# Attention's query tiles in a one-core hybrid block: who writes their constant rows

## The chip, the cores and the metric

The kernel runs on one core of one Trainium2 chip. The metric is device time in microseconds of one execution. Before the change three timed executions took 3047.77, 3050.18 and 3064.09 us; the median, 3050.18 us, is the time that the change is measured against.

## The reference

One layer over 16 meta tokens and 2048 frames of width 1024: an RMS norm and an input projection, three groups of heads side by side (RG-LRU, forgetting attention, RWKV-7), an output projection with norm and residual, then a gated feed-forward network. The part that matters here is the attention, 8 heads of 64:

```python
c = jnp.cumsum(log_f, axis=1)                       # log forget gates, summed over time
s = einsum('bhqd,bhkd->bhqk', qb, kh) + (cb[..., :, None] - c[..., None, :])
s = jnp.where(kpos[None, :] <= qpos[:, None], s, -jnp.inf)
p = jax.nn.softmax(s, axis=-1)
o = einsum('bhqk,bhkd->bhqd', p, vh)
```

## The kernel before, in words

The program has four stages on one core. Stage one multiplies the normed input by the input weights and runs the two recurrences beside it (class Rwkv and the LRU). Its last projection matmul is at 890 us of the span. Stage two is the attention (class `Attn`), from there to about 1580 us, with the rest of the recurrences and most of the output projection beside it. Stage three is the first half of the feed-forward network, stage four its second half.

Every matrix product of float32 values is done in parts: a value is split into a rounded high part and a low rest, and the products of the parts are summed. For attention this is packed into the contraction dimension of 128 partitions. A score tile (`sc`, lines 681 and 682) is the sum of two matmuls, `k1` by `q1` and `k2` by `q2`. A maximum tile (`mx`, line 554) is one matmul, `q3` by `k2`, of which only the row maximum is used. Partitions 0 to 63 of `q3` and `q2` hold a head's queries. Partitions 64 to 127 hold constants or zero: in `q3` partition 64 is 0, partitions 65 and 66 are 1 (they add the two parts of the forget sum that stand in the same partitions of `k2`), and the rest is 0. In `q2` all are 0 at first, and partition 64 later gets the negative row maximum from ScalarE (line 568). In `k2` partition 64 is 1, partitions 65 and 66 are loaded, and the rest is 0.

These tiles are allocated once, in `Attn.__init__`, as rings of three `q3`, three `q2` and two `k2`, and reused for all 32 steps (8 heads by 4 blocks of 512 queries), so the constant rows are written once. VectorE writes them for the queries: lines 476, 477 and 478 in the helper `fixed` for each `q3` (64 partitions of 0, then 3 of 1, then 1 of 0) and line 462 for each `q2`. GpSimd writes them for `k2` (lines 480 and 481).

A step is made of `maxima` (up to five `mx` pieces for each of four query tiles, each followed by a VectorE row maximum at line 559; then a reduction at 564, transposes at 567 and the ScalarE operation at 568) and `weights` (scores, exponentials at line 686, sums and values). `maxima` runs two steps ahead of `weights` (`AHEAD = 2`).

The order of instructions within each engine isn't the order of the code. A scheduler in the framework plays the program through and gives each engine a list that it then runs in that order; every DMA named here is issued by SyncE (SP), in order as well. So the recurrences and the attention are merged on every engine, and an instruction that is taken away lets the scheduler place all that follows anew.

The names that the prediction uses beside these: `rwst` is the recurrence's state, which line 1267 (VectorE) copies and line 1263 (TensorE) multiplies, four times in turn for each block of 256 frames; `rwix` at line 78 is the last of a square root's steps and the input of the matmul at line 1067; `rwraw` (line 996) is a load of projection rows for the next block of the recurrence, and line 1006 (ScalarE) and 1007 (VectorE) read it; `rww` at line 1313 is the normed output of a recurrence block, which line 1320 (TensorE) transposes; line 1179 is the recurrence's triangular solve, whose results go through VectorE (lines 1189, 1195, 1202) and come back.

Of the kernel before, what the change touches and what calls it, by code (L numbers as in the profile page):

```python
# [8 lines left out]
F32 = mybir.dt.float32  # L9
# [3 lines left out]
AF = mybir.ActivationFunctionType  # L13
# [5 lines left out]
P = 128  # L19
# [13 lines left out]
class Core:  # L33


    def __init__(self, tc, ctx):
        self.tc = tc
        self.nc = tc.nc
        self.ctx = ctx
        self.uid = 0  # L40
        nc = self.nc
        self.const = ctx.enter_context(tc.tile_pool(name="const", bufs=1))
        self.ident = self.const.tile([P, P], F32, name="ident")
        make_identity(nc, self.ident[:])
        self.flip = 0
        self.root = self.apart = False
# [310 lines left out]
def attn_consts(core):  # L357
    nc = core.nc
    c = core.const

    core.future = c.tile([META, META], F32, name="future")
    core.futureb, core.identb = (c.tile([P, P], BF16, name=s) for s in ("futureb", "identb"))
    for t, n in ((core.future, META), (core.futureb, P)):
        nc.gpsimd.memset(t[:], 0.0)
        nc.gpsimd.affine_select(
            out=t[:], in_=t[:], compare_op=ALU.is_ge, fill=NEG, base=0, pattern=[[-1, n]], channel_multiplier=1
        )
    nc.vector.tensor_copy(core.identb[:], core.ident[:])
    core.ones_row = c.tile([1, P], F32, name="ones_row")
    nc.vector.memset(core.ones_row[:], 1.0)  # L370
    core.ccol = c.tile([P, NKT, NH], F32, name="ccol")
    nc.vector.memset(core.ccol[:], 0.0)
    core.cref = c.tile([P, NKT, NH], F32, name="cref")
    core.ncref = c.tile([1, NKT, NH], F32, name="ncref")
    core.ctail = c.tile([NH, META], F32, name="ctail")
    nc.vector.memset(core.ctail[:], 0.0)
    core.ones_col = c.tile([P, 1], F32R, name="ones_col")
    nc.vector.memset(core.ones_col[:].bitcast(F32), 1.0)
    core.ones_64 = c.tile([META, 64], F32, name="ones_64")
    nc.vector.memset(core.ones_64[:], 1.0)  # L380
    core.ones_8 = c.tile([NH, 1], F32, name="ones_8")
    nc.vector.memset(core.ones_8[:], 1.0)

# [55 lines left out]
class Attn:  # L439
# [7 lines left out]
    def __init__(self, core, pool, psum, more, scr):  # L447
        self.core, self.pool, self.psum, self.more, self.scr = core, pool, psum, more, scr
        self.wide, self.bank, self.place = False, 0, 0
        nc = self.nc = core.nc  # L450
        self.clock, self.later, self.serial, self.added = 0, [], 0, 0
        self.pending, self.loads, self.steps, self.beside = None, [], [], iter(())


        self.turn = {"k": 1, "q2": 0, "q3": 0}
        self.ring = {s: [] for s in self.turn}
        for i in range(self.AHEAD + 1):
            q3 = pool.tile([P, 512], F32R, tag=f"q3_{i}", name=core.n("q3"), bufs=1)
            self.fixed(q3, None, self.ONES)
            self.ring["q3"].append(q3)  # L460
            q2 = pool.tile([P, 512], F32R, tag=f"q2_{i}", name=core.n("q2"), bufs=1)
            nc.vector.memset(q2[64:128].bitcast(F32), 0.0)
            self.ring["q2"].append(q2)
            if i > 1:
                continue
            k1 = pool.tile([P, 2, KHALF], F32R, tag=f"k1_{i}", name=core.n("k1"), bufs=1)
            k2 = pool.tile([P, 2, KHALF], F32R, tag=f"k2_{i}", name=core.n("k2"), bufs=1)
            v1 = pool.tile([P, 2, NKT // 2 + 1, 64], F32, tag=f"v1_{i}", name=core.n("v1"), bufs=1)
            self.fixed(None, k2, self.ONES)
            self.ring["k"].append((k1, k2, v1))  # L470
# [1588 lines left out]
def hybrid_block_kernel(ctx: ExitStack, tc: tile.TileContext, args, out):  # L2059
# [25 lines left out]
    with ExitStack() as p1:  # L2085
# [7 lines left out]
        with ExitStack() as p1a:  # L2093
# [6 lines left out]
            for part in range(3):  # L2100
# [9 lines left out]
                if part == 0:  # L2110
                    attn_consts(core)
                    rk = rwkv_consts(
                        core, gp, ps_ae,
                        {
                            s[5:]: (v.rearrange("h d -> (h d)") if s == "rwkv_r_k" else v)
                            for s, v in a.items() if s.startswith("rwkv_")
                        },
                    )
                    lk = lru_consts(
                        core, gp, ps_ae,  # L2120
                        {
                            "conv_w": a["lru_conv_w"], "conv_b": a["lru_conv_b"], "ga_w": a["lru_gate_a_w"],
                            "ga_b": a["lru_gate_a_b"], "gx_w": a["lru_gate_x_w"], "gx_b": a["lru_gate_x_b"],
                            "lam": a["lru_lambda"],
                        },
                    )
                    columns(core, gp, ps_ae, [a["ffn_conv"].rearrange("i (r p) -> (i r) p", p=P)], "", cw)
                    R = Rwkv(core, rp, dp, ps_rw, ps_ae, scr, rk)
                    beside = Beside(PACE)
# [190 lines left out]
```

## Time and profile before

| | |
|---|---|
| three timed executions, us | 3047.77, 3050.18, 3064.09 |
| the profiled execution, us | 3044.26 |
| its span, first to last instruction, us | 3042.5 |
| granted TensorE clock, mean | 0.977 |
| TensorE busy, 890 to 940 us | 36.36 of 50 us |
| TensorE busy, 1300 to 1400 us | 97.00 of 100 us |
| VectorE busy, 890 to 940 us | 42.56 of 50 us |

How to read the lines of the profile: in a timeline row come the start in us, the duration in us, engine, line, operation, output and inputs with their sizes, the count, and in brackets how long the engine stood idle before it and what ended that. In a table by windows come, for each stretch of time, the busy microseconds and instruction counts of TensorE (PE), its weight loads (PEld), VectorE (DVE), ScalarE (ACT) and GpSimd (POOL), the granted TensorE clock, the share in which the DMA engines were busy, and what they moved in GB/s. Rows of a line's own view give the shortest, median and longest duration in ns, and the first and last start. A row of waits gives total, count and longest.

### The profile page before, as it was taken

The page shows a single profiled execution, that of the slowest core. Times are in us where ns is not written, and L with a number is a line of the kernel's source. Part 1 is how long each engine was busy: PE and PEld are TensorE (multiplying, and loading weights), DVE is VectorE, ACT ScalarE, POOL GpSimd, SP SyncE. Part 2 cuts the span into 40 slices and gives each one's busy share as a digit, 9 for nine tenths or more (in the row PEclk, how much of TensorE's full clock was granted, in tenths as well). Part 3 has the DMA queues.
Part 4 walks back from the last instruction along what each step waited for, and adds up shares of the span by engine and source line. Part 5 has one row for each costly group of instructions (what it writes and reads, how often), then busy time and mean ns, then how long its engine had stood idle before and what let it go on. Part 6 is the DMA issues. An engine that isn't in the chain of part 4 may idle for free. (4 is left out here: it accounts for less than half of the span.)

```text
span 3042.5 us, 52754 instructions
## 1 busy us (share of the span) xinstructions
PE 2901.8 (95%) x18694; PEld 2486.7 (82%) x18694; DVE 2043.7 (67%) x3947; ACT 1480.9 (49%) x2858; POOL 1309.2 (43%) x1567
## 2 busy tenths in 40 slices
PE   6998999999989998999989899999999999999998
PEld 6998898888876654565568899999999999787887
DVE  5268645656677885555736888888778777646666
ACT  4245342434346654454634656666666665434333
POOL 1001121122224656566843457545655544556443
PEclk9998999999998999999999999999999999999999
DMA  6776478565654347434326555567677764536453
GB/s 211 245 233 214 155 237 294 159 212 193 213 160 95 97 102 214 110 94 123 82 81 221 166 168 181 180 187 221 210 220 208 216 204 130 167 109 213 146 182 120
DMA packets 469189, 530.48 MB, mean 174 GB/s; under 512 B 85710, under 2 KB 355736, under 8 KB 467372
## 3 DMA queue, kind: packets, MB, share of 16 engines
q1 hardware_dynamic: 468156, 526.17, 56.6%
q8 instruction: 147, 2.41, 0.3%
q0 software_dynamic: 768, 0.93, 0.1%
q14 instruction: 118, 0.97, 0.1%
HBM read 368.07 MB, written 158.90 MB: 173 GB/s over the span
## 5 line engine op out<-in xcount | busy, mean ns | idle before, releaser
L172 PE MATMUL psu<-xo,uw 128*128 128x344 f32 x1848 | 591.3, 324 | 15.6 <-DVE vb L1812 7.9
L173 PE MATMUL psu<-xo,uw 128*128 128x344 f32 x1848 | 593.9, 322 | 0.0
L174 PE MATMUL psu<-xo,uw 128*128 128x344 f32 x1848 | 585.0, 321 | 0.7 <-DVE uw L1621 0.7
L172 PE MATMUL psp<-xh,wh 128*128 128x384 f32 (+2 forms) x1152 | 382.9, 332 | 4.2 <-ACT wh L166 3.1
L174 PE MATMUL psp<-xh,wl 128*128 128x384 f32 (+2 forms) x1152 | 380.3, 331 | 2.0 <-DMA wl<-scr_wk 1.8
L173 PE MATMUL psp<-xl,wh 128*128 128x384 f32 (+2 forms) x1152 | 379.5, 330 | 0.0
L172 PEld LDWEIGHTS psu<-xo,uw 128*128 128x128 f32 x1848 | 348.1, 189 | 19.1 <-DVE vb L1812 9.9
L1621 DVE TENSOR_TENSOR uw<-uq,uw 128x512 fp32r<-128x512 f32 x341 | 316.9, 936 | 67.9 <-ACT uw L1620 65.8
L173 PEld LDWEIGHTS psu<-xo,uw 128*128 128x128 f32 x1848 | 349.2, 189 | 0.0
L174 PEld LDWEIGHTS psu<-xo,uw 128*128 128x128 f32 x1848 | 347.7, 189 | 1.3 <-DVE uw L1621 1.2
L1620 ACT ACTIVATE uw<-uq 128x512 fp32r<-128x512 f32 x462 | 287.0, 627 | 105.0 <-PE psu L174 47.8
L686 ACT ACTIVATE p<-sc,bias 128x512 f32<-128x512 f32 (+4 forms) x352 | 197.4, 590 | 191.3 <-PE sc L682 159.1
L559 DVE TENSOR_REDUCE mc<-mx 128x1 f32<-128x512 f32 (+6 forms) x352 | 190.3, 564 | 105.2 <-PE mx L554 79.9
L1760 DVE SCALAR_TENSOR_TENSOR uy<-psu,ffn_cols,uy 128x342 f32<-128x342 f32 (+1 forms) x390 | 220.2, 566 | 57.4 <-ACT uy L1758 55.7
L1768 POOL TENSOR_TENSOR uy<-uy,uy 128x342 f32<-128x342 f32 (+1 forms) x132 | 139.3, 1056 | 249.8 <-DVE uy L1760 63.7
L1621 POOL TENSOR_TENSOR uw<-uq,uw 128x512 fp32r<-128x512 f32 x121 | 180.9, 1495 | 148.4 <-ACT uw L1620 130.5
L725 POOL TENSOR_TENSOR acc<-acc,p 128x512 f32<-128x512 f32 (+3 forms) x208 | 221.2, 1066 | 52.3 <-DVE acc L725 26.3
L174 PEld LDWEIGHTS psp<-xh,wl 128*128 128x128 f32 x1152 | 221.3, 192 | 11.5 <-issue 6.0
L172 PEld LDWEIGHTS psp<-xh,wh 128*128 128x128 f32 x1152 | 221.4, 192 | 11.0 <-issue 4.0
L173 PEld LDWEIGHTS psp<-xl,wh 128*128 128x128 f32 x1152 | 221.2, 192 | 7.7 <-issue 5.6
L1621 DVE TENSOR_TENSOR fo<-u,fo 128x896 fp32r<-128x896 f32 x88 | 100.1, 1138 | 132.7 <-ACT fo L1620 132.2
L1620 ACT ACTIVATE fo<-u 128x896 fp32r<-128x896 f32 x88 | 81.2, 923 | 207.1 <-PE psd L174 115.6
(483 smaller groups left out, 6399.2 us busy)
## 6 DMA issues: line engine op xcount, KB each, us to landing
uq<-scr_us SPq DMA_DIRECT2D x220, 256.0 KB
uq<-in_ffn_up_dram SPq DMA_DIRECT2D x209, 256.0 KB
wl<-scr_wk SPq DMA_DIRECT2D x48, 512.0 KB
wh<-scr_wk SPq DMA_DIRECT2D x48, 512.0 KB
u<-scr_ff SPq DMA_DIRECT2D x88, 256.0 KB
scr_ff<-uy SPq DMA_DIRECT2D x110, 171.0 KB
raw<-in_w_in_dram SPq DMA_DIRECT2D x24, 512.0 KB
scr_wk<-wh SPq DMA_DIRECT2D x24, 512.0 KB
```

The source lines that it names most:

```text
L172: nc.tensor.matmul(out, ah, bh, start=first, stop=False, skip_group_check=more)
L173: nc.tensor.matmul(out, ah, bl, start=False, stop=False, skip_group_check=more)
L174: nc.tensor.matmul(out, al, bh, start=False, stop=last, skip_group_check=more)
L559: self.reduced = nc.vector.tensor_reduce(mc[:rows, i, ci : ci + 1], ps[:rows, : e - a], axis=AX.X, op=ALU.max)
L686: last = nc.scalar.activation(p[:rows, :w], ps[:rows, :w], AF.Exp, bias=bias[:rows, j : j + 1])
L725: eng.tensor_tensor(a, ps_[0][0][:rows, c0:n] if start and i == 1 else a, p[:rows, : n - c0], op=ALU.add)
L1620: core.nc.scalar.activation(hi, src, AF.Copy)
L1621: (eng or core.nc.vector).tensor_tensor(lo, src, hi, op=ALU.subtract)
L1760: core.conved = stt(y[:, :n], src[:, i : n + i], cw[:, 44 * i + cc : 44 * i + cc + 1], y[:, :n], op0=ALU.mult, op1=ALU.add)
L1768: core.pooled = nc.gpsimd.tensor_tensor(v[:, :n], g[:, :n], v[:, :n], op=ALU.mult)
```

## The change

`attn_consts` gets a column of 128 values, `qrows`, written by three VectorE memsets of one column at the start of the program: 0 everywhere, 1 in partitions 64 to 66, 0 in partition 64. In `Attn.__init__` the three memsets of each `q3` give way to one ScalarE operation that multiplies any finite input by 0 and adds the column as its bias. The memset of each `q2` moves from VectorE to GpSimd. `fixed` stays, for the `k2` tiles and for the 16 meta tokens.

```diff
+    core.qrows = c.tile([P, 1], F32, name="qrows")
+    for rows, value in ((slice(0, P), 0.0), (slice(64, 64 + Attn.ONES + 2), 1.0), (slice(64, 64 + Attn.ONES), 0.0)):
+        nc.vector.memset(core.qrows[rows], value)
...
             q3 = pool.tile([P, 512], F32R, tag=f"q3_{i}", name=core.n("q3"), bufs=1)
-            self.fixed(q3, None, self.ONES)
+            nc.scalar.activation(
+                q3[64:128], core.ident[64:128, 0:1].to_broadcast([64, 512]), AF.Identity, scale=0.0,
+                bias=core.qrows[64:128],
+            )
             self.ring["q3"].append(q3)
             q2 = pool.tile([P, 512], F32R, tag=f"q2_{i}", name=core.n("q2"), bufs=1)
-            nc.vector.memset(q2[64:128].bitcast(F32), 0.0)
+            nc.gpsimd.memset(q2[64:128].bitcast(F32), 0.0)
```

The lines of the changed kernel are numbered 3 higher from line 381 on and 6 higher from line 463 on. Up to the start of the attention the order of every engine is that of before, but for the three small memsets and a few constants set around them. From there to about 1500 us of the span the scheduler has placed much anew; behind that, the orders are the same again. Three places follow.

VectorE where the attention begins, before. The names `q_1455`, `q_1460` and `q_1465` are the three `q3`; `q_1456`, `q_1461` and `q_1466` are the three `q2`; `mc` collects maxima.

```order
L1267 COPY rwst_9235<-rps_9237 128x128
L476 MEMSET q_1455_11123 64x512
L462 MEMSET q_1456_11127 64x512
L476 MEMSET q_1460_11134 64x512
L462 MEMSET q_1461_11138 64x512
L476 MEMSET q_1465_11145 64x512
L77 TENSOR_TENSOR rwitmp_9683<-rwitmp_9683,rwia_9681 4x256
L462 MEMSET q_1466_11149 64x512
L547 MEMSET mc_11168 128x20
L547 MEMSET mc_11204 128x20
L1267 COPY rwst_9235<-rps_9237 128x128
L477 MEMSET q_1455_11123 3x512
```

The same place of the changed kernel, with line 1273 for 1267 and 1075 for 1069.

```order
L1273 COPY rwst_9239<-rps_9241 128x128
L553 MEMSET mc_11166 128x20
L553 MEMSET mc_11202 128x20
L77 TENSOR_TENSOR rwitmp_9687<-rwitmp_9687,rwia_9685 4x256
L78 SCALAR_TENSOR_TENSOR rwix_9686<-rwitmp_9687,rwix_9686 4x256
L1273 COPY rwst_9239<-rps_9241 128x128
L1176 STREAM_TRANSPOSE rwxu_9972<-rwxu_9972 64x512
L1075 SCALAR_TENSOR_TENSOR rwk_9660<-rwk_9660,rwkv_cols,eps_9773 128x256 x2
```

The twelve memsets (five more of them stand behind the rows shown) are gone, and the second state copy has moved up past all those that stood ahead of it. The three ScalarE operations stand behind the last rounding of the projection (line 234), ahead of the three bias operations (line 570 before, 576 now). The three GpSimd memsets stand among those of `k2`: one `q2`, one `k2`, and so on, and then the rows of 1.

SyncE in the same stretch, before: the query loads of the third step, the values, the keys of the next head, and then the recurrence's `rwraw`.

```order
L541 DMA q_1455_11123<-scr_qh 64x512
L542 DMA q_1495_11264<-scr_qh 64x512
L543 DMA q_1495_11264<-scr_qh 64x512
L544 DMA q_1456_11127<-scr_ql 64x512
L523 DMA v_1459_11131<-scr_v 128x8x64
L524 DMA v_1459_11131<-scr_v 16x64
L523 DMA v_1459_11131<-scr_v 128x8x64
L524 DMA v_1459_11131<-scr_v 16x64
L515 DMA k_1463_11141<-scr_kh 64x1040
L517 DMA k_1463_11141<-scr_ch 1x1040
L518 DMA k_1463_11141<-scr_cl 1x1040
L996 DMA rwraw_10432<-scr_p 128x2x65
```

The changed kernel, with line 1002 for 996, 525 and 526 for 519 and 520, 547 for 541.

```order
L525 DMA k_1457_11131<-scr_kh 64x1040
L1002 DMA rwraw_10436<-scr_p 128x2x65
L526 DMA k_1457_11131<-scr_kl 64x1040
L547 DMA q_1455_11127<-scr_qh 64x512
L548 DMA q_1495_11262<-scr_qh 64x512
L549 DMA q_1495_11262<-scr_qh 64x512
L550 DMA q_1456_11129<-scr_ql 64x512
L529 DMA v_1459_11133<-scr_v 128x8x64
```

`rwraw` has moved up by twelve loads, past the third step's queries and the values.

TensorE at the recurrence's first triangular solve within the attention, before.

```order
L1179 MATMUL rps_10039<-rwxu_9968,rwsc_8714 32x32 x32
L554 MATMUL mx_11381<-k_1458_11130,q_1460_11134 128x400
L554 MATMUL mx_11384<-k_1458_11130,q_1460_11134 128x512
L556 LDWEIGHTS identb
L556 MATMUL mx_11384<-futureb,identb 128x128
L681 MATMUL sc_11462<-q_1495_11264,k_1457_11129 128x512
L682 MATMUL sc_11462<-q_1456_11127,k_1458_11130 128x512
L681 MATMUL sc_11468<-q_1495_11264,k_1457_11129 128x400
L682 MATMUL sc_11468<-q_1456_11127,k_1458_11130 128x400
L1179 MATMUL rps_10073<-rwxu_9968 32x32 x16
```

The changed kernel, with line 1185 for 1179, 560 for 554, 573 for 567, 687 and 688 for 681 and 682.

```order
L1185 MATMUL rps_10043<-rwxu_9972,rwsc_8718 32x32 x32
L573 MATMUL mx_11312<-ident,sh_11310 1x128 x4
L560 MATMUL mx_11337<-k_1458_11132,q_1460_11136 128x400
L687 MATMUL sc_11414<-q_1477_11197,k_1457_11131 128x272
L688 MATMUL sc_11414<-q_1466_11147,k_1458_11132 128x272
L687 MATMUL sc_11420<-q_1477_11197,k_1457_11131 128x144
L688 MATMUL sc_11420<-q_1466_11147,k_1458_11132 128x144
L1185 MATMUL rps_10077<-rwxu_9972 32x32 x16
```

The solve stands earlier among the attention's rows, and between its first two parts stand 1,744 streamed columns where 2,864 stood.

## Prediction

> **What bounds the kernel now.** I read the page's table of busy time first.
>
> ```profile
> span 3042.5 us, 52754 instructions
> PE 2901.8 (95%) x18694; PEld 2486.7 (82%) x18694; DVE 2043.7 (67%) x3947; ACT 1480.9 (49%) x2858; POOL 1309.2 (43%) x1567
> ```
>
> TensorE is busy for 95% of the span, so an edit on VectorE counts only where TensorE waits for it. The second view is the table by windows around 890 us, where the attention begins.
>
> ```profile
> 896.00:900.00 4.00, 0.90 (x10) 0.71 (x10) 3.35 (x10) 0.00 (x0) 3.15 (x2) 0.72 1.00 238
> 900.00:904.00 4.00, 2.84 (x6) 1.66 (x6) 3.49 (x9) 0.00 (x0) 0.00 (x0) 0.50 0.91 215
> 904.00:908.00 4.00, 4.00 (x38) 2.70 (x37) 3.44 (x10) 0.00 (x0) 0.00 (x0) 0.50 0.91 227
> ...
> 916.00:920.00 4.00, 2.76 (x10) 2.25 (x11) 3.17 (x15) 2.46 (x5) 0.53 (x3) 0.50 1.19 210
> 920.00:924.00 4.00, 3.98 (x20) 2.75 (x19) 3.90 (x8) 2.08 (x6) 3.61 (x8) 0.80 1.15 213
> 892.00:928.00 36.00, 23.68 (x200) 16.86 (x196) 30.68 (x85) 8.08 (x17) 11.69 (x14) 0.76 0.96 198
> 925.00:1580.00 655.00, 609.04 (x3635) 375.84 (x3635) 414.49 (x942) 345.24 (x669) 410.38 (x573) 0.96 0.43 110
> ```
>
> From 892 to 928 us TensorE does 23.68 of 36 us, at a mean clock of 0.76, while VectorE is busy for 30.68 and the DMA engines are full. This seam is bound by VectorE and by the loads, not by TensorE. From 925 to 1580 us TensorE stands idle for 655 - 609.04 = 46 us; there it is the bound. The third view is the timeline of TensorE in the seam.
>
> ```profile
> 898.15 0.70 PE L1263 MATMUL rps<-rwst,rwgt 64*64 64x64 f32 x8 [3.79 <-DVE rwst L1267]
> 901.16 2.07 PE L1067 MATMUL eps<-rwix,spr 4*128 4x256 f32 x4 [2.11 <-DVE rwix L78]
> 907.40 0.91 PE L554 MATMUL mx<-k,q 128*128 128x144 f32 x1
> 917.24 0.58 PE L554 MATMUL mx<-k,q 128*128 128x256 f32 x1 [2.66 <-ACT q L568]
> ```
>
> Two waits of 3.79 and 2.11 us end on the state copy and on the square root, both on VectorE. The fourth view says what VectorE did instead.
>
> ```profile
> L476 DVE MEMSET q<- x3: 485/485/485, 894.0 to 896.2; 64x512 f32 x3
> L462 DVE MEMSET q<- x3: 485/485/485, 894.6 to 897.3; 64x512 f32 x3
> L477 DVE MEMSET q<- x3: 485/485/485, 898.3 to 900.2; 3x512 f32 x3
> L478 DVE MEMSET q<- x3: 485/485/485, 901.3 to 902.8; 1x512 f32 x3
> 897.83 0.27 DVE L1267 COPY rwst<-rps 128x128 f32<-128x128 f32 x1
> 900.69 0.41 DVE L78 SCALAR_TENSOR_TENSOR rwix<-rwitmp,rwix 4x256 f32<-4x256 f32 x1
> ```
>
> A memset of 1 partition takes as long as one of 64. The twelve sit exactly between the copies and the root that TensorE waits for.
>
> **The change part by part: what goes.** VectorE loses 12 x 0.485 = 5.82 us in the seam. TensorE's two waits there are 3.79 + 2.11 = 5.90 us, so the two views agree on the size: what follows can come forward by 5.8 us at most. Whether it does depends on what is late next.
>
> ```profile
> 894.25 0.47 SPq L515 DMA_DIRECT2D k<-scr_kh  x1
> k<-scr_kh SPq DMA_DIRECT2D x8, 260.0 KB
> q<-scr_qh SPq DMA_DIRECT2D x13, 128.0 KB
> ```
>
> First, the loads. The first maxima (907.40 us) need `k2` and `q3`; ahead of them in the queue lie two loads of 260 KB and, as long again, the low part, then 128 KB: 908 KB beside the small rows. The first is issued at 894.25; at the 238 GB/s of the window from 896 us that is 3.8 us, so some time about 899 to 901 us. The maxima would come at 907.40 - 5.8 = 901.6 us. The loads allow it, with little to spare.
>
> Second, ScalarE's part of the step, which now is late for another reason.
>
> ```profile
> 909.29 0.91 ACT L1006 ACTIVATE rwrav<-rwraw,rwkv_om 128x256 f32<-128x256 f32 x2 [18.12 <-PE rps L1295]
> 916.14 0.35 ACT L1006 ACTIVATE rwwa<-rwraw,rwkv_om 128x64 f32<-128x64 f32 x1 [2.13 <-DMA rwraw<-scr_p]
> 916.51 0.68 ACT L568 ACTIVATE q<-mx,ncref 1x512 fp32r<-1x512 f32 x1
> 912.00 0.38 SPq L996 DMA_DIRECT2D rwraw<-scr_p  x1
> rwraw<-scr_p SPq DMA_DIRECT2D x1, 65.0 KB
> ```
>
> The row maximum at 916.51 us, on which the first full scores depend, stands behind a ScalarE operation that waits for `rwraw`, loaded 4.1 us after its issue. If that load stayed at 912.00, the gain would end here. It doesn't: it has moved up past twelve loads on SyncE, 65 KB ahead of the low keys and the third step's queries. Those are wanted well behind 917 us, so I count the move itself at nothing.
>
> Third, TensorE's new order. The transposes of line 1320 now stand ahead of the scores with 272 columns, and they need the recurrence's normed output.
>
> ```profile
> 920.41 1.53 DVE L1313 TENSOR_TENSOR rww<-rww,rwgsm 128x512 f32<-128x512 f32 x1
> ```
>
> VectorE reaches that product only behind a chain of ten small operations and several row maxima. Before, six score and maximum matmuls more stood ahead of the transposes. I take 1.5 us, the length of that product, as newly exposed. The bounds are 0, if the maxima cover it, and 3 us, twice the row. So the seam gives 5.8 - 1.5 = 4.3 us, between 2.8 and 5.8.
>
> **What comes.** Three ScalarE operations over 64x512, and three GpSimd memsets.
>
> ```profile
> L748 ACT ACTIVATE oh<-acc x32: 612/618/632, 936.1 to 1565.7; 128x512 fp32r<-128x512 f32 x32
> L1165 POOL MEMSET rwxu<- x9: 195/523/527, 12.0 to 1059.4; 64x512 f32 x8, 64x128 f32 x1
> 895.55 3.60 POOL L481 MEMSET k<- 1x2080 f32 x2
> ```
>
> ScalarE's nearest row is 0.618 us, so 1.9 us for the three; they lie in the 18.12 us for which ScalarE stands idle ahead of 909.29. Without that cover they would cost 1.9 us, but no queue is behind them there. On GpSimd three memsets of 0.523 us delay the last constants of `k2` from 899.15 to 900.7 us. The first maxima wait for those, at 901.6 us in the sum above: covered by 0.9 us, at most 1.6 us if the cover is gone. The three memsets of one column at the program's start cost VectorE a fraction of a microsecond while loads are awaited. All this is counted at nothing.
>
> **The new order behind the seam.** About 570 us of attention run in another order. It has the same work, and TensorE's idle 46 us are the sum of many short waits.
>
> ```profile
> PE sc L681 <- ACT p L686: 9.5, 18, 2.0
> PE mx L554 <- DVE mc L559: 7.2, 9, 2.7
> PE mx L751 <- ACT oh L748: 7.0, 2, 4.7
> ```
>
> Whether a wait of this kind falls away or comes new can't be read from the order. I take 0, and as bounds one of these three groups more or less, 9.5 us either way. The handover to the feed-forward network has the order of before, so a gain reaches the end unshortened.
>
> **The sum.** The profiled execution took 3044.3 us; less 4.3 is 3040.0. The median lies 5.9 us above it, and I expect the changed kernel's runs to do likewise: 3045.9 us, a gain of 0.14%. A measurement of this kernel tells apart about 0.5%, 15 us.
>
> **One rule weighed.** The granted clock falls to 0.72 in the window with the 3.79 us wait and to 0.50 in the next. The Trainium skill (TensorE: Matmul & The Clock Gate, section "Part 1: The HAM clock gate (the "warmup" mystery)") says that a window of about 3.4 us without activity halves TensorE's clock and a busy one of that length restores it. The trace agrees. By that rule the seam without its waits would run at full clock, and the sum would be the second rival's. I don't count it, since TensorE then waits for its first keys for about as long.
>
> **The rivals.** *The loads take over* (3050 us): TensorE gets ready earlier and then waits for keys and queries; for it speaks a DMA share of 0.91 to 1.19 in the windows shown from 896 to 924 us, against it the 899 to 901 us worked out above. The gain is then under 1 us.
>
> *The clock stays up* (3039 us): the whole 5.8 us, and the 2.84 + 4.00 us of matmuls between 900 and 908 us, granted 0.50, run at twice the clock, which saves 3.4 us; the 2.76 us between 916 and 920 save 1.4 more. 3050.2 - 10.6 = 3039.6. Against it speaks the wait for the first loads.
>
> *The recurrence in TensorE's way* (3062 us): the solve now stands earlier, with 1,744 columns instead of 2,864 between its first parts, and TensorE runs in order.
>
> ```profile
> 948.28 3.19 PE L1179 MATMUL rps<-rwxu 32*32 32x32 f32 x96 [1.65 <-DVE rwxu L1189]
> ```
>
> Three blocks of the recurrence are left, with about ten such turns each through VectorE or ScalarE. Should ten of thirty become exposed at 1.65 us, that costs 16.5 us, and 3045.9 + 16.5 = 3062. It eats the gain from three exposed turns on (4.3 / 1.65). Against it: over the whole first solve the columns between its parts come to about the same, some are thinner and some thicker.
>
> *The operation is not free* (3048 us): the ScalarE form calls for a table load, 1.28 us each at line 1431, and the `q3` are late. The lists of both kernels hold 52 table loads and none at this place, so this is all but excluded.
>
> ```profile
> L1431 ACT ACT_TABLE_LOAD  x18: 1283/1283/1283, 214.2 to 1049.1; - x18
> ```
>
> **How the numbers follow.** Forecast (3041 to 3050) 0.50, loads 0.20, recurrence 0.16, clock 0.12, operation 0.02. The range goes from the clock's 3039 less most of the 9.5 us of the order, 3032, up to 3060: the forecast plus 9.5 and the spread of the three timings, without the worse part of the recurrence's case. Faster by over 0.5% means below 3034.9: only the clock's case with luck in the order, or the forecast with all of it, 0.11. Slower means above 3065.4: a third of the recurrence's case and a bad order, 0.09. That leaves 0.80 for the same.
>
> **What would show it.** Right: the four state copies lie under 2 us apart, TensorE's first maxima start before 903 us, the row maximum on ScalarE before 912 us, and the attention's last stage starts 4 us earlier. Wrong: the first maxima behind 905 us with no VectorE wait ahead (the loads); waits of line 1185 on VectorE over 5 us in total (the recurrence); TensorE's idle time from 925 us on more than 10 us off 46 (the order decides, not the memsets).

## The result, and the profile after

The changed kernel took 3064.93 us in the median of 13 runs (3052.22 to 3071.56), before took 3047.59 us in 13 runs beside them (3042.67 to 3064.09). The ratio on record, which isn't that of the two medians, is 1.0043, with a 95% interval from 1.0028 to 1.0057: about 13 us slower. (The medians alone lie 17.3 us apart, a ratio of 1.0057.) The changed kernel's median lies above the range that was predicted, 3032 to 3060 us.

The table of busy time of the changed kernel, and the windows that answer to those shown of before:

```profile
span 3064.0 us, 52768 instructions
PE 2913.1 (95%) x18694; PEld 2491.5 (81%) x18694; DVE 2039.8 (67%) x3938; ACT 1483.7 (48%) x2861; POOL 1307.7 (43%) x1570
```

```profile
904.00:908.00 4.00, 4.00 (x46) 2.40 (x46) 3.09 (x8) 0.00 (x0) 0.87 (x1) 0.50 0.83 202
916.00:920.00 4.00, 3.50 (x12) 2.81 (x13) 3.07 (x9) 2.18 (x4) 1.19 (x4) 0.50 1.03 205
892.00:928.00 36.00, 30.10 (x248) 21.84 (x246) 30.07 (x83) 11.05 (x25) 13.89 (x19) 0.72 0.76 173
925.00:1580.00 655.00, 603.89 (x3571) 370.58 (x3572) 416.16 (x930) 342.36 (x662) 399.36 (x553) 0.94 0.42 106
```

TensorE has the same matmuls and is busy 11 us longer: a busy microsecond at a lower clock does less. From 925 to 1580 us its clock is 0.94 where it was 0.96, and it is idle for 51 us where it was 46.

The two runs have to be laid over each other first. In the run after, the last projection matmul ends at 894.45 us, in the one before at 890.11; the order up to there is the same, so these 4.3 us belong to the run. All times from here on that are called "behind the seam" count from that matmul. The seam, on TensorE, on VectorE's state copy and on ScalarE:

```profile
898.97 1.13 PE L1073 MATMUL eps<-rwix,spr 4*128 4x256 f32 x4 [0.37 <-DVE rwix L78]
903.36 2.08 PE L1094 MATMUL eps<-rwsq,bones 128*128 128x512 f32 x2 [2.78 <-DVE rwk L1075]
909.56 0.49 PE L560 MATMUL mx<-k,q 128*128 128x144 f32 x1
```

```profile
897.82 0.27 DVE L1273 COPY rwst<-rps 128x128 f32<-128x128 f32 x1
898.84 0.27 DVE L1273 COPY rwst<-rps 128x128 f32<-128x128 f32 x1
901.85 0.70 DVE L1176 STREAM_TRANSPOSE rwxu<-rwxu 64x512 f32<-64x512 f32 x1 [2.74 <-DMA rwxu<-dx]
903.37 1.58 DVE L1273 COPY rwst<-rps 128x128 f32<-128x128 f32 x1
```

```profile
894.90 1.94 ACT L462 ACTIVATE q<-ident,qrows 64x512 fp32r<-64x512 f32 x3
908.63 0.91 ACT L1012 ACTIVATE rwrav<-rwraw,rwkv_om 128x256 f32<-128x256 f32 x2 [11.02 <-PE rps L1301]
915.77 0.68 ACT L574 ACTIVATE q<-mx,ncref 1x512 fp32r<-1x512 f32 x1 [1.30 <-PE mx L573]
```

The wait of 2.11 us has shrunk to 0.37, that of 3.79 is gone (the state's copies wait for no memset any more); a new one of 2.78 has come. That one ends on line 1075, which stands on VectorE right behind the operation of line 1176, and this had waited 2.74 us for a load: with the memsets gone, VectorE gets to `rwxu` before its data do. ScalarE's first row maximum (line 574) starts 21.3 us behind the seam, where it started 26.4 us behind it: 5.1 us gained. By ScalarE's first `oh` (line 754), which closes the first step of the weights, the gain is gone (46.3 us behind the seam after, 46.0 before), and by the first matmul of the feed-forward network the changed kernel is 16.9 us behind (801.8 against 784.9). From there to the end the distance stays. The waits of TensorE from 925 to 1580 us, in us in total, count and longest:

```profile
PE mx L560 <- DMA k<-scr_cl: 12.2, 6, 4.2
PE mx L573 <- DVE sh L570: 8.7, 6, 4.5
PE sc L687 <- ACT p L692: 7.7, 23, 0.9
PE mx L560 <- DVE mc L565: 6.5, 11, 1.5
PE eps L1054 <- ACT rwe L1045: 2.1, 1, 2.1
```

The waits for keys (5.0 before) and for the maxima's reduction at line 570 (2.0 before) have grown by 7 us each; those for the exponentials have shrunk from 9.5, and 7.0 us of waits for `oh` are gone. In sum TensorE's idle time has grown by 5 us, which doesn't make 17. The first 120 us from about the first `oh` on, of before and of the changed kernel, show more in the clock: 0.93 against 0.80.

```profile
935.00:1055.00 120.00, 110.70 (x1148) 76.26 (x1148) 97.99 (x267) 77.82 (x170) 65.42 (x112) 0.93 0.35 87
```

```profile
939.00:1059.00 120.00, 108.25 (x1052) 74.03 (x1050) 85.67 (x236) 64.87 (x142) 54.41 (x95) 0.80 0.30 73
```

**A sum that closes.** From tables by windows of 1 us between the seam and the feed-forward network I add up what TensorE is idle (1 less busy) and what it is throttled (busy times 1 less clock). What is left of the stretch is work at full clock. In the twenty profiles of this study it is 689 to 698 us: the work is nearly the same everywhere, and most of the difference between the slow kernels and before lies in the two other columns. (Of the lead of e3, e4 and e15, the kernels faster than before, some 3 to 4 us lie in this rest, which stays unexplained.)

| kernel (one profile each) | ratio to before, 95% interval | seam to network | idle | throttled | rest |
|---|---|---|---|---|---|
| before | 1 | 784.9 | 58.8 | 30.9 | 695.2 |
| changed | 1.0043 (1.0028 to 1.0057) | 801.8 | 62.5 | 46.3 | 693.0 |
| e1 ScalarE half | 0.9985 (0.9970 to 1.0000) | 782.2 | 55.9 | 28.8 | 697.5 |
| e2 GpSimd added | 0.9992 (0.9978 to 1.0006) | 799.2 | 59.8 | 45.3 | 694.0 |
| e5 change, old order | 1.0001 (0.9988 to 1.0014) | 784.5 | 59.2 | 29.6 | 695.8 |
| e6 old work, new order | 1.0054 (1.0034 to 1.0075) | 803.1 | 63.3 | 45.1 | 694.7 |
| e7 zeros last | 1.0042 (1.0026 to 1.0058) | 798.6 | 64.3 | 39.2 | 695.1 |
| e3 GpSimd half | 0.9970 (0.9952 to 0.9987) | 779.7 | 55.7 | 32.5 | 691.5 |
| e15 change, third order | 0.9981 (0.9968 to 0.9994) | 780.1 | 59.7 | 28.1 | 692.3 |
| e4 all by ScalarE | 0.9980 (0.9966 to 0.9995) | 781.3 | 52.4 | 38.0 | 690.9 |
| e8 first wait away | 1.0032 (1.0020 to 1.0044) | 799.1 | 65.8 | 38.7 | 694.6 |
| e9 second wait away | 1.0034 (1.0019 to 1.0049) | 799.4 | 65.5 | 37.9 | 696.0 |
| e10 both away | 1.0034 (1.0019 to 1.0049) | 805.0 | 62.1 | 49.9 | 693.1 |
| e11 wait put in | 1.0016 (1.0002 to 1.0031) | 802.0 | 62.4 | 46.7 | 693.0 |
| e12 new, then old order | 1.0034 (1.0021 to 1.0047) | 801.8 | 61.0 | 46.1 | 694.8 |
| e13 old, then new order | 1.0034 (1.0020 to 1.0047) | 797.9 | 60.3 | 44.3 | 693.3 |
| e14 new order, 100 us | 1.0039 (1.0024 to 1.0054) | 795.6 | 55.5 | 45.3 | 694.9 |
| e17 q3 by GpSimd | 1.0019 (1.0006 to 1.0033) | 797.5 | 60.4 | 42.5 | 694.6 |
| e18 zeros twice | 1.0002 (0.9989 to 1.0015) | 795.1 | 58.1 | 41.7 | 695.2 |
| e16 three idle memsets | 1.0244 (1.0226 to 1.0263) | 867.2 | 101.8 | 76.0 | 689.4 |

One profile is one run: before and e2 have the same order to 19 TensorE rows and the same time, and e2's profile happens to hold 14 us more throttling, nearly as much as the changed kernel's. So a single row of this table decides nothing. Verdicts come from the ratios; the columns, averaged, say what a difference is made of. In the mean, the three profiles of the new order (changed, e6, e7) against the four of the old one (before, e1, e2, e5): 63.4 against 58.4 us idle, 43.5 against 33.7 throttled. The granted clocks of all runs, not only of the profiled ones, agree. The span times what the clock lacks to 1, idle time included, is 70.7 us in the mean of the 23 runs of before that stand beside e5 to e7, and 71.3 us in the 12 of e5. In the new order it is 82.7 us in the 6 of e6 and 80.3 in the 12 of e7. That is 10 to 12 us more, of the 13 to 17 us by which these two kernels' spans are longer.

### The profile page after: what moved, and what is told of

Its sections match the earlier page's. It is cut to its first block, busy times and chain, and to the rows that moved or that the text cites. A ratio compares the mean times of both kernels' runs of the same rounds, so it can differ in the third digit from the quotient of the medians.

```text
span 3064.0 us, 52768 instructions
## 1 busy us (share of the span) xinstructions
PE 2913.1 (95%) x18694; PEld 2491.5 (81%) x18694; DVE 2039.8 (67%) x3938; ACT 1483.7 (48%) x2861; POOL 1307.7 (43%) x1570
## 4 chain that ended last, share of the span: by engine, by line
PE 70%; DVE 10%; DMA 9%; ACT 4%; issue 3%; POOL 3%; SPq 1%; DVEq 0%; ACTq 0%; POOLq 0%
PE psu L172 9%; PE psu L173 9%; PE psu L174 9%; PE psd L172 4%; PE psd L173 4%; PE psd L174 4%; PE po L710 4%; PE psp L174 3%; PE psp L173 3%; PE psp L172 3%; PE mx L560 2%; PE pswo L172 2%; PE pswo L174 2%; PE pswo L173 2%; PE sc L687 2%
## 5 line engine op out<-in xcount | busy, mean ns | idle before, releaser
L1766 DVE SCALAR_TENSOR_TENSOR uy<-psu,ffn_cols,uy 128x342 f32<-128x342 f32 (+1 forms) x390 | 220.6, 567 | 60.7 <-ACT uy L1764 59.2
```

The costliest lines, as they stand in the source:

```text
L1766: core.conved = stt(y[:, :n], src[:, i : n + i], cw[:, 44 * i + cc : 44 * i + cc + 1], y[:, :n], op0=ALU.mult, op1=ALU.add)
```

## The experiments

The theories. A: the loss is the new order behind the seam, whatever the operations. B: the moved operations cost. C: VectorE's relief itself does harm.

**The halves (e1 to e4).** The edits, against the changed kernel in e1 and e4, against before in e2 and e3:

```diff
# e1
-            nc.gpsimd.memset(q2[64:128].bitcast(F32), 0.0)
+            nc.vector.memset(q2[64:128].bitcast(F32), 0.0)
# e2
+            nc.gpsimd.memset(q2[64:128].bitcast(F32), 0.0)
             nc.vector.memset(q2[64:128].bitcast(F32), 0.0)
# e3
-            nc.vector.memset(q2[64:128].bitcast(F32), 0.0)
+            nc.gpsimd.memset(q2[64:128].bitcast(F32), 0.0)
# e4
-            nc.gpsimd.memset(q2[64:128].bitcast(F32), 0.0)
+            nc.scalar.activation(q2[64:128], core.ident[64:128, 0:1].to_broadcast([64, 512]), AF.Copy, scale=0.0)
```

> The ScalarE half alone: the q3 rows come from ScalarE, the q2 zeros stay on VectorE. Nine of the twelve memsets leave VectorE, yet the order behind the seam is nearly that of before (21 of some 16,300 TensorE matmul rows stand elsewhere, all within the first 300 rows of the attention). Theory A (the loss of 13 us is the new order behind the seam): this kernel costs no more than before; at best it keeps the seam's gain of 2 to 4 us, so 3043 to 3048 us on the chip of the first comparison, ratio 0.9985 to 1.0005. Theory B (the ScalarE operations themselves are what costs): most of the loss is here already, ratio 1.002 to 1.005. Theory C (loss because VectorE's copies now come before other work): nine of twelve memsets gone should bring about three quarters of it, ratio 1.003.

> Before, with the three GpSimd memsets of the q2 zeros added ahead of VectorE's own (which stay). The order of TensorE is that of before but for 19 rows. It has the GpSimd work of the change and none of its relief. Theory A: GpSimd's 1.6 us delay the last k2 rows by as much, at a place where TensorE waits for loads as well: 0 to 1.6 us, ratio 0.9995 to 1.0005. Theory B' (the GpSimd operations cost, by holding VectorE up or by late k2 rows): ratio 1.002 or more.

> The GpSimd half alone: the q2 zeros move to GpSimd, q3 stays with VectorE as before. Only three of twelve memsets leave VectorE (1.5 us), but the order behind the seam is a third one: 1,254 TensorE rows stand elsewhere than before, and 1,024 elsewhere than in the changed kernel. Theory A: the time is whatever this order gives, and the size of the edit says nothing; a spread of 10 us either way, ratio 0.997 to 1.004, and the profile's waits of TensorE behind 930 us with its throttled time account for it. Theory B/B': the work moved is a quarter, so the difference is under 1.5 us or a quarter of 13 us, ratio 0.9995 to 1.001.

> All constant rows of the queries by ScalarE (the q2 zeros too, multiplied by 0); GpSimd gets nothing, VectorE loses all twelve memsets. Another order again (2,077 TensorE rows elsewhere than before, 1,831 elsewhere than in the changed kernel). Theory A: its own time, anywhere within 10 us of before, ratio 0.997 to 1.004, not tied to that of the changed kernel. Theory B: at least the loss of the changed kernel, as ScalarE has twice the operations: ratio 1.004 or more. Theory C (VectorE's relief itself makes it slower): the same as the changed kernel, 1.004.

Measured: 0.9985, 0.9992, 0.9970 and 0.9980. None of them is slower than before. B falls with e1, e2 and e4, which hold each operation of the change and more; C falls with e4, where VectorE loses all twelve memsets. (e1 and e2 run nearly in the order of before, e4 in one of its own; e5 below answers both theories again, in the order of before.) e3, which takes three memsets of 0.485 us off VectorE, gains 0.30%, about 9 us: six times what it moves.

**The orders exchanged (e5 to e7).** In e5 and e6 each engine's list is pinned by edges without semaphores, from the list of instruction numbers of the other kernel:

```diff
+def pin_order(tc, nc):
+    for chain in json.loads(zlib.decompress(base64.b85decode(_ORDER))).values():
+        for first, then in zip(chain, chain[1:]):
+            tc.add_manual_dep(
+                nc.get_inst_by_name(f"I-{then}"), f"I-{first}",
+                mybir.DependencyInfo(mybir.DependencyClass.NoSync, mybir.DependencyReason.DATA), reason="order",
+            )
```

In e7 the GpSimd memsets of `q2` stand behind the loop.

```diff
-            nc.gpsimd.memset(q2[64:128].bitcast(F32), 0.0)
...
+        for q2 in self.ring["q2"]:
+            nc.gpsimd.memset(q2[64:128].bitcast(F32), 0.0)
```

> The changed kernel's instructions, all of them, in the order of before: every engine's list from the seam to about 1500 us is pinned to that of before by order edges without waits; only the three ScalarE operations and three GpSimd memsets stand where the scheduler puts them (ahead of the first maxima), and the twelve VectorE memsets are gone. Theory A (the loss of 13 us is the order alone): no loss, at best the seam's gain as in the ScalarE half: ratio 0.997 to 1.0005. Theory B (the operations cost, in ways that the halves alone did not show, for instance both together): 1.002 to 1.005.

> The reverse: the instructions of before, with all twelve memsets on VectorE at the seam, and every engine's list from the seam on pinned to the order of the changed kernel. Theory A: the loss is here although nothing of the change is, with the memsets' few us on top or hidden: ratio 1.003 to 1.007. Theory B (operations): no loss, 0.999 to 1.001.

> The changed kernel with its three GpSimd memsets of the q2 zeros behind those of k2 instead of between them; the orders of TensorE, VectorE and ScalarE are those of the changed kernel to the last row, on GpSimd and SyncE one or two rows stand elsewhere. The k2 constants come 1.6 us earlier. Theory A: the time of the changed kernel, ratio 1.003 to 1.0055. If the late k2 constants hold the first maxima: 1.6 us less at most plus what follows from it, under 1.002 only if the start of the attention were what loses the 13 us.

Measured: 1.0001, 1.0054 and 1.0042. This settles it: the whole change in the old order costs nothing, and the old instructions, all twelve memsets among them, lose in the new order what the changed kernel loses. The traces bear the edit out: from the seam to the network TensorE's 4,297 rows stand in e5 exactly as in before, and in e6 exactly as in the changed kernel. The pinning itself costs nothing that shows, as e5 is pinned too. The same 120 us from the first `oh` on, of e5, e6 and e7:

```profile
935.00:1055.00 120.00, 111.36 (x1145) 77.07 (x1145) 95.92 (x266) 77.77 (x170) 64.71 (x110) 0.91 0.35 86
```

```profile
935.00:1055.00 120.00, 107.57 (x1076) 75.04 (x1074) 89.36 (x247) 68.12 (x149) 56.40 (x99) 0.84 0.29 73
```

```profile
935.00:1055.00 120.00, 106.35 (x1071) 74.31 (x1070) 89.43 (x246) 68.00 (x149) 56.70 (x99) 0.84 0.29 73
```

In the new order TensorE is busy for 4 to 5 us less, and at a clock of 0.84 instead of 0.91. e5 also shows that the old order doesn't let the seam's gain through: its first row maximum starts 26.4 us behind the seam, as before.

**Two waits taken away, one put in (e8 to e11).** The new order has waits that return to 0.02 us. In the changed kernel, in e6 and in e7, on TensorE:

```profile
971.85 0.59 PE L1054 MATMUL eps<-rwsq,gat 128*4 128x64 f32 x4 [2.08 <-ACT rwe L1045]
1013.05 1.01 PE L573 MATMUL mx<-ident,sh 128*1 128x128 f32 x4 [4.46 <-DVE sh L570]
```

```profile
967.71 0.39 PE L1048 MATMUL eps<-rwsq,gat 128*4 128x64 f32 x4 [2.08 <-ACT rwe L1039]
1005.11 1.01 PE L567 MATMUL mx<-ident,sh 128*1 128x128 f32 x4 [4.46 <-DVE sh L564]
```

```profile
968.34 0.59 PE L1055 MATMUL eps<-rwsq,gat 128*4 128x64 f32 x4 [2.08 <-ACT rwe L1046]
1006.66 1.01 PE L574 MATMUL mx<-ident,sh 128*1 128x128 f32 x4 [4.44 <-DVE sh L571]
```

e8 to e10 pin the changed kernel to its own order with these places mended, e11 pins it to the order of before with the first wait put in:

```diff
# e8, TensorE: the two L1054 matmuls behind the next L1234 x4, L573 x4, L560, L562;
#     VectorE: L570 ahead of L1439, and L1056, L74, L1070 behind L1235
# e9, VectorE: L570 ahead of L770, L747, L1316
# e10: both
# e11, TensorE, order of before: the two L1054 matmuls ahead of the fifteen rows behind L1043
```

> The changed kernel in its own order, with one place mended: two matmuls of a 64-column norm (line 1054) that wait 2.08 us for ScalarE in all three profiles of this order stand twelve TensorE rows later, behind rows that are ready, and VectorE's maxima reduction of that step stands ahead of the operation that reads their result (ten VectorE rows change places). Nothing is taken away. Theory A1 (the order costs through a few fixed waits, each of which also halves TensorE's clock for a time): the wait of 2.1 us goes and with it the throttled stretch behind it, worth 5.1 to 9.4 us in the three profiles: 7 to 11 us less than the changed kernel, ratio to before 1.0005 to 1.002. Theory A2 (waits alone count, the clock comes back by itself elsewhere): 2 us less, ratio 1.0035 to 1.0045. Theory A3 (a wait taken away only comes back further down): no difference, 1.004 to 1.005.

> The changed kernel in its own order, with the other place mended: one VectorE reduction of 4 columns (line 570), for which TensorE's transposes wait 4.4 to 4.5 us in all three profiles, moves up past three operations, among them an operation of 8 columns that takes 3.1 us there instead of 0.17. Theory A1: 4 us of waiting and 2.3 to 4.0 us of throttling go: 6 to 8 us less, ratio to before 1.0015 to 1.0025. Theory A2: 4 us less, 1.003. Theory A3: no difference.

> The changed kernel in its own order with both places mended. Theory A1: 13 to 19 us less than the changed kernel, so the whole loss and perhaps more: ratio to before 0.998 to 1.0005. Theory A2: 6 us less, ratio 1.002 to 1.003. Theory A3: no difference, 1.004.

> The changed kernel's instructions in the order of before (which ran at ratio 1.0001), with the first of these waits put in: the same two matmuls moved up by fifteen rows, right behind the matmuls whose result ScalarE must take out first, so that TensorE has about 2 us to wait there. Theory A1: 2 us and a throttled stretch of 3.4 to 9.4 us: 4 to 11 us more, ratio 1.0015 to 1.004. Theory A2: 2 us, 1.0005 to 1.001.

Measured: 1.0032, 1.0034, 1.0034 and 1.0016. My theory A1 falls for the waits taken away: 6 to 19 us should have come back, and about 3 did (1.0043 to 1.0033), with intervals that overlap that of the changed kernel. A3 is what the profiles show. In e8 the wait has moved to the next rows:

```profile
966.50 1.97 PE L1234 MATMUL rps<-rww,rwxf 64*64 64x128 f32 x8 [2.54 <-ACT rww L1236]
971.16 1.97 PE L1249 MATMUL rps<-rwsc,rwxu 64*64 64x128 f32 x16 [0.98 <-ACT rww L1236]
```

because its source is not the row that waits. ScalarE, in the changed kernel, has two table loads around a square root right ahead of what TensorE needs:

```profile
967.93 1.28 ACT L1437 ACT_TABLE_LOAD   x1
969.23 0.42 ACT L1437 ACTIVATE rwlr<-rwlr 128x256 f32<-128x256 f32 x1
969.66 1.28 ACT L1065 ACT_TABLE_LOAD   x1
970.96 0.31 ACT L1065 ACTIVATE rwe<-rwe 128x128 f32<-128x128 f32 x1
971.28 0.52 ACT L1045 ACTIVATE rwe<-eps,rwkv_om 128x64 f32<-128x64 f32 x2
```

The old order has the same square root and the same two loads (in e5 at 970.19 and 971.92 us); ten value matmuls and four score matmuls happen to be ready for TensorE there. In e9 the wait of 4.46 us became 0.23 and 3.41, the second for the reduction behind the same slow VectorE operation:

```profile
1006.78 0.60 PE L573 MATMUL mx<-ident,sh 128*1 128x128 f32 x4 [0.23 <-DVE sh L570]
1012.02 0.70 PE L560 MATMUL mx<-k,q 128*128 128x400 f32 x1 [3.41 <-DVE mc L565]
```

e11 did what A1 says, in size at its lower edge: 1.0016 against 1.0001 for the same instructions without the wait, though the intervals overlap. In its profile the wait of 1.96 us is followed by some 13 us at half clock, with TensorE busy throughout (the windows from its start on):

```profile
972.00:976.00 4.00, 2.39 (x14) 1.86 (x15) 1.95 (x7) 2.34 (x9) 0.07 (x1) 0.76 0.08 29
976.00:980.00 4.00, 4.00 (x23) 3.17 (x23) 2.22 (x8) 3.00 (x7) 1.01 (x3) 0.50 0.16 45
980.00:984.00 4.00, 4.00 (x27) 2.90 (x24) 2.68 (x10) 0.35 (x1) 0.44 (x1) 0.50 0.00 0
984.00:988.00 4.00, 4.00 (x42) 3.13 (x41) 2.03 (x9) 0.76 (x2) 0.68 (x3) 0.54 0.17 16
```

where e5, without the wait, has

```profile
974.00:978.00 4.00, 4.00 (x47) 3.13 (x44) 3.74 (x14) 3.58 (x10) 0.66 (x2) 1.00 0.06 16
```

The third step's `oh` then stands at 101.2 us behind the seam instead of 92.7. Of these 8.5 us 0.8 were there ahead of the wait, so one wait of 2 us cost between 7 and 8 in this profile.

**Where in the order (e12 to e14), and the best version (e15).** Hybrids of the two lists, cut where ScalarE writes the seventh or the third `oh`, and the change in the order of e3.

```diff
# e12: new order up to the seventh oh, then what is left, in the old order
# e13: old order up to the seventh oh, then what is left, in the new order
# e14: new order up to the third oh, then what is left, in the old order
# e15: all instructions of the change, in the order of e3
```

> The changed kernel's instructions, pinned: the new order from the seam to the seventh step of the weights (about 170 us behind the seam), and from there all that is left in the order of before. Theory P1 (the loss arises in these 170 us, where the three profiles of the new order fall 16 to 18 us behind, and the rest neither adds nor gives back): ratio 1.003 to 1.0055. Theory P2 (the loss is spread over the whole 570 us, and the drift at 170 us is only work put off): 1.0005 to 1.002. Theory P3 (it lies behind): 0.999 to 1.0005.

> The counterpart: the order of before up to the seventh step of the weights, and behind it what is left in the new order. Theory P1: 0.9985 to 1.001. Theory P2: 1.001 to 1.003. Theory P3: 1.003 to 1.0055.

> The new order only up to the third step of the weights (about 100 us behind the seam), then that of before. In the three profiles the new order is 8 to 11 us behind by then. Theory P1: half to two thirds of the loss, ratio 1.0015 to 1.0035. Theory P2: under 1.001. If the loss needs the second hundred us: 0.999 to 1.0005.

> All instructions of the change, pinned to the order of the kernel with the GpSimd half alone, the fastest so far (ratio 0.997). Theory A (the order sets the time): 0.9955 to 0.9985, faster than before and than the changed kernel, with the seam's 2 to 4 us on top at best. If the operations of the change cost in any order: 1.000 or more.

Measured: 1.0034, 1.0034, 1.0039 and 0.9981. P1, P2 and P3 all fall: either half of the new order loses about as much as the whole (the intervals overlap), and its first 100 us alone do too. The parts don't add up, and each hybrid is also an order of its own, with a break in it. Which places of the new order lose the 13 us stays open. e15 answers the other question: the operations of the change allow a kernel that is faster than before, and add no gain that shows to what the order gives (0.9981 against 0.9970 for e3, the fastest version here).

**How far orders lie apart (e16 to e18).**

```diff
# e16, before
+        self.spare = pool.tile([P, 512], F32, tag="spare", name=core.n("spare"), bufs=1)
...
             nc.vector.memset(q2[64:128].bitcast(F32), 0.0)
+            nc.vector.memset(self.spare[64:128], 0.0)
# e17, before
-            self.fixed(q3, None, self.ONES)
+            for rows, value in ((64, 0.0), (3, 1.0), (1, 0.0)):
+                nc.gpsimd.memset(q3[64 : 64 + rows].bitcast(F32), value)
# e18, changed
             nc.gpsimd.memset(q2[64:128].bitcast(F32), 0.0)
+            nc.vector.memset(q2[64:128].bitcast(F32), 0.0)
```

> Before, with three useless VectorE memsets of 64x512 added (one for each query tile, into a tile that nobody reads). By the arithmetic of the seam this costs 1.5 us, ratio 1.0005. The order behind the seam is a new one (1,928 TensorE rows elsewhere than before). If the order decides: its own time, anywhere from 0.997 to 1.005, and TensorE's idle and throttled time between the seam and the feed-forward network, summed, stands above or below the 85 to 90 us of before by about as much.

> Before, with the nine q3 memsets moved to GpSimd and the q2 zeros left on VectorE. Another order that the scheduler makes by itself (1,221 TensorE rows elsewhere than before, 693 elsewhere than in the changed kernel). GpSimd has 4.7 us more work ahead of the k2 constants. If the operations decide: k2's constants come 3 us later than in the changed kernel, 1.001 to 1.002 above before, or the seam's gain of 2 us. If the order decides: anywhere from 0.997 to 1.005, nearer to the changed kernel's 1.0043 if likeness of order counts.

> The changed kernel, with VectorE's three q2 memsets back behind those of GpSimd. VectorE loses nine memsets instead of twelve. Another order of the scheduler's own (1,011 TensorE rows elsewhere than before, 875 elsewhere than in the changed kernel). If the operations decide: as the ScalarE half, 0.9985 to 1.0005. If the order decides: anywhere from 0.997 to 1.005.

Measured: 1.0244, 1.0019 and 1.0002. e17 and e18 lie between the others. e16 is far outside what I had allowed: three memsets that nobody needs, 1.5 us of VectorE, cost 75 us, with the new order that the scheduler made around them. Its first `oh` comes 197 us behind the seam instead of 46, the recurrence runs nearly alone until then, and all of the loss is in idle and throttled time. Whether the 1.5 us or the tile of 2 KB a partition made the scheduler do that was not taken apart, so e16 says nothing on memsets. It says how far a small edit can reach.

## Why the prediction was wrong, point by point

*What goes, in the seam* (4.3 us, 2.8 to 5.8): right in size. The first row maximum came 5.1 us earlier behind the seam, in e7 5.9 us. The path was not quite the one I gave: the first maxima came only 2.2 us earlier (15.1 us behind the seam instead of 17.3), since TensorE then waited 2.78 us for line 1075, which a load of the recurrence, `rwxu`, had held up on VectorE. The prediction looked at the loads of keys, queries and `rwraw` only. The rest came from ScalarE, no longer held by `rwraw`: its load is issued 16.4 us behind the seam instead of 21.9, the move on which the prediction had made the gain depend. Of its signs of being right only the row maximum came true (911.4 us on the clock of before); the first maxima stood at 905.2 us instead of before 903, and the state copies lay up to 4.5 us apart.

*What comes*: right. The ScalarE operations took 1.94 us and were followed by 11.02 us of idleness; the delay on GpSimd is worth nothing that shows (e7, 1.0042). Nor do the operations cost anything in the old order (e5, 1.0001).

*The new order behind the seam* ("I take 0, and as bounds one of these three groups more or less, 9.5 us either way"): this is the step that failed. From the first row maximum to the network the stretch grew from 758.5 us to 780.5; over the four profiles of the old order and the three of the new one the means are 762 and 779: 17 us, against a bound of 9.5. Two things were wrong in it. The bound took one wait group for the size of the whole; the eight orders that the scheduler made by itself (before, changed, e1 to e4, e17, e18) gave 0.997 to 1.0043, a ninth (e16) 1.0244. And it counted waiting alone: of the 15 us between the mean sums above, 5 are idle time and 10 are throttling. What stays open is which places of the order make them.

*The rule weighed*: I weighed the clock in the seam alone, and there only as a possible gain. Behind the seam the sum has no term for it, and there it makes about two thirds of the loss. The prediction also took a window of about 3.4 us without activity as what halves the clock; here waits of 1.96 us (e11) and 1.52 us (the changed kernel, below) were enough.

*The handover*: right, with the other sign. The loss of 16.9 us at the first matmul of the network, measured from the seam, reached the end.

*The rivals*: from 925 us on the recurrence's waits at line 1185 came to 0.9 us on VectorE, so that rival was not it. That its 3062 us lie near the measured time is luck. The clue that I named for "the order decides, not the memsets", idle time more than 10 us off 46, would have missed: idle time moved by 5. The clue looked at waiting alone, as the bound did.

## What to carry to other kernels

Where a scheduler lays out the program, the price of an edit is that of its operations plus that of a new order, and the second can be the larger by far; pin the instructions of one kernel to the order of the other, both ways, before explaining anything by what was moved. A wait of TensorE can cost its length and the clock behind it (in e11's profile 7 to 8 us for 2). Moving the row that waits doesn't help if the engine that it waits for is the one that is stalled; look for the table load or the slow operation ahead of the releaser.

## What the runs showed of the hardware that I had not expected

**What runs behind a wait goes with its price.** In thirteen profiles (before, changed, e1 to e11) I listed every stretch from 925 to 1705 us with the clock below 1. Of 163, 88 last 3.4 us at a loss of 1.4 to 1.7 us; matmuls with tiles of fewer than 128 rows or 64 columns are 0% of the matmul time in them, in the median. One of them, behind a wait of 1.52 us in the changed kernel:

```profile
1236.00:1240.00 4.00, 4.00 (x11) 1.31 (x11) 2.85 (x8) 2.18 (x3) 2.43 (x3) 0.57 0.03 6
1240.00:1244.00 4.00, 3.83 (x24) 2.43 (x20) 2.67 (x5) 2.44 (x5) 3.35 (x8) 1.00 0.51 130
```

The 22 longest last 10 to 21 us at a loss of 3.9 to 9.4 us, and such narrow matmuls, mostly the recurrence's, are 56% in the median. The plainest case is e16: 17.45 of 18 us busy, almost wholly with matmuls whose tiles are 64 by 64, and the clock doesn't rise; nor does it in 160 us around them, of which TensorE is busy for 115.

```profile
1012.00:1030.00 18.00, 17.45 (x146) 15.95 (x145) 8.20 (x27) 7.04 (x15) 6.93 (x10) 0.50 0.02 4
920.00:1080.00 160.00, 114.78 (x1145) 94.87 (x1144) 88.19 (x285) 46.60 (x105) 24.43 (x43) 0.50 0.13 30
```

The same holds over all twenty profiles from 100 to 1700 us. A stretch of 7 us in which TensorE is busy for 96% or more, less than a fifth of it with narrow matmuls, ends at half clock in 15 of 16,718 cases, counted in steps of 1 us. With more than four fifths narrow it does in 22 of 26, nearly all of them in e16. No run changed the width of the matmuls alone, so that the width is the cause is not shown.

The Trainium skill (TensorE: Matmul & The Clock Gate, section "Part 1: The HAM clock gate (the "warmup" mystery)") says that a busy window of about 3.4 us restores the full clock. The trace agrees for the wide matmuls (full clock behind nearly all busy stretches of 7 us) and differs for these narrow ones (17.45 of 18 us busy at 0.50). The page also says that the window runs freely and that how long a kernel's start runs at the lower clock varies with it from run to run; the 14 us more of throttling in e2's profile, in the order of before, go with that, though no run here shows the cause.

**An operation of 8 columns that takes 3.1 us.** Line 1316, in the changed kernel, lasts 0.17 us in the median of nine and 3.09 us once, where GpSimd adds sums beside it:

```profile
L1316 DVE TENSOR_SCALAR rwgsm<-rwgsm x9: 161/171/3094, 366.2 to 1136.5; 128x8 f32<-128x8 f32 x8, 64x4 f32<-64x4 f32 x1
```

It ends with the last of the sums, at 1012.92 and 1012.90 us:

```profile
1009.83 3.09 DVE L1316 TENSOR_SCALAR rwgsm<-rwgsm 128x8 f32<-128x8 f32 x1
1009.56 1.02 POOL L731 TENSOR_TENSOR acc<-p,p 128x400 f32<-128x400 f32 x1
1010.55 2.35 POOL L731 TENSOR_TENSOR acc<-acc,p 128x272 f32<-128x272 f32 x4
```

Its longest is 3.09 us in e6 and e7 as well, and the wait of 4.4 to 4.5 us behind it is the one shown above. The Trainium skill (SBUF — State Buffer, section "Who interferes with whom") says that VectorE and GpSimd share a pair of ports as an exclusive lock. The trace agrees with that in the common end, 0.02 us apart; here the wait lasted over five GpSimd instructions, not one. No run took the sums away, so the lock as its cause is likely and not shown.
